# Forward substitution in the RWKV scan of a bidirectional hybrid encoder layer: one series of VectorE operations for two blocks of tokens

## The chip, the cores and the metric

The kernel runs on one core of a Trainium2 chip. A core has five engines that run on their own: TensorE (PE; its weight loads are shown apart as PEld), VectorE (DVE), ScalarE (ACT), GpSimd (POOL) and SyncE (SP). Each works off its own list of instructions in order. DMAs are issued by SP, ACT and POOL and run beside the engines. The metric is the device time of one execution in microseconds (us); lower is better.

## The reference, cut to what matters

One layer of an encoder over 1024 tokens of width 1024, all in float32: half-step SwiGLU feed-forward, a mixing layer, a second half-step feed-forward. The mixing layer projects the tokens once, gives eight heads to a dilated attention and eight heads to an RWKV-7 recurrence that runs over the tokens forward and backward. Only the recurrence bears on the change:

```python
def _rwkv7_step(state, inp):
    r, w, k, v, kk, kka = inp
    sa = jnp.einsum('dbhvk,dbhk->dbhv', state, kk)
    state = state * w[..., None, :] - sa[..., :, None] * kka[..., None, :] + v[..., :, None] * k[..., None, :]
    y = jnp.einsum('dbhvk,dbhk->dbhv', state, r)
    return state, y
...
    _, ys = lax.scan(_rwkv7_step, state0, xs)      # 1024 steps, both directions
    y = ys[:, :, 0] + jnp.flip(ys[:, :, 1], axis=1)
```

The state is 64 by 64 for each head and direction. Then each head is normalised, a bonus is added, the result is gated, and it is joined with the attention for the output projection.

## The kernel before, in words

The kernel is written against a layer that takes the program in the order in which Python issues it, gives each tile a buffer of its pool (a pool has so many buffers for each tag, and a tile waits for the readers of the buffer's last owner), and then orders the instructions of each engine by priority, which follows the program's order, and by when its own model of the times holds them ready. So an engine's list mixes instructions of several steps, and on the chip it is worked off in order.

Feed-forward 1, the input projection and the attention come first, then the scan stage (about 1240 to 1640 us of the execution), then the output projection and feed-forward 2.

The scan is cut in 16 chunks of 64 tokens for each direction; two chunks make a block, so there are 8 blocks of 128 tokens (`NB`). Both directions and eight heads of a block are worked on together. Four steps make a block n:

- `prep` (L783): for each direction it loads the block's decay, in-context rates and projections, takes exponentials (L805, L806 on ACT), forms the products `pr` (L810, L811) and `bk` (L814 to L822) on DVE, multiplies them on PE (L830) and masks the result into `lm` on DVE (L832, eight instructions to a block). `lm` holds the triangular matrices of the block. Four DMAs on SP write the two 32 by 32 diagonal pieces of each to a scratch tensor in DRAM (L846), in an order in which partition means one matrix.
- `solve` (L850): two DMAs on SP load them into `X`, 128 matrices on 128 partitions, each 32 by 32 (L856). POOL clears `Ti` and sets its diagonal (L860, L862). Then 31 steps of forward substitution invert all of them: each step is a multiply (L866) and a subtract (L868) on DVE over r x m elements to a partition, r = 31 - s, m = s // 2 + 1; each waits for the one before. A copy (L870) makes the transpose in `X`, and four DMAs on POOL write both to DRAM (L872, L873).
- `merge` (L875): six DMAs on POOL bring the inverses back in the layout of the matrices (L883, L886), PE multiplies them with the off-diagonal pieces (L894, L900) and ACT copies the result to `tt` (L902).
- `chain` (L918): the sequential part. For each of the two chunks PE multiplies with the carried state (L941, L952, L937), DVE scales the new state (L968), and ACT copies the outputs `yb` (L970), which are stored at the end (L972). The last L970 of a block ends its chain.

The tiles that `prep` hands on (`lm`, `gc`, `pr`, `bt`) come from two pools: `B0` with two buffers for blocks 1, 2, 4, 5 and 7, and `R0` with one for blocks 0, 3 and 6. So block n + 3 takes the buffers of block n, and its `pr` (L810) and `lm` wait for the last matmul of block n's chain. `X`, `Ti` and the scratch tile `ttmp` have two buffers each.

The order in which the program issues the steps is in `run`: block 0's `prep` and `solve`, then `upto(1)` (prep and solve of block 1), the merge of block 0, `upto(2)`, and then for each block n: merge, chain, `upto(n + 3)`, and the output products of the attention for one tile of tokens (`project_attended`, L1066: loads and a multiply L1072, a split L1078, 24 matmuls L1064). Where the scan ends, `finish_unit` (L975) takes over: it adds the directions, normalises and gates.

Of the kernel before, what the change touches and what calls it, by code (L numbers as in the profile page):

```python
# [10 lines left out]
F32 = mybir.dt.float32  # L11
F32R = mybir.dt.float32r
AF = mybir.ActivationFunctionType
OP = mybir.AluOpType
# [17 lines left out]
def _ap(src, off, pat):  # L32
    return bass.AP(tensor=src.tensor, offset=src.offset + off, ap=pat)
# [3 lines left out]
class _GateUp:  # L37
# [3 lines left out]
    def __init__(self, K, ring, rows, w, hid, wd, ws):  # L41
        self.K, self.ring, self.rows, self.w, self.hid, self.wd, self.ws = K, ring, rows, w, hid, wd, ws
        self.A, self.S, self.P, self.X, self.H = {}, {}, {}, {}, {}
        self.ready, self.done = {}, set()
# [38 lines left out]
    def gather(self, n, j):  # L83
# [3 lines left out]
        if n == 1:  # L87
            self.X[j] = [self.rows.tile([128, 2, 512], F32, name="row", tag="row") for q in range(2)]
        x, y = self.X[j]
        if n == 1:  # L90
# [73 lines left out]
class _Kernel:  # L164
# [454 lines left out]
    def far(self, psum, p, h, q, k, v3):  # L619
# [8 lines left out]
        s = p.tile([128, NT, 64], F32, name="sb3", tag="sb3", bufs=1)  # L628
        V.tensor_reduce(out=n3[:, :, 64], in_=ps, op=OP.max, axis=AX.X)
        V.tensor_tensor(s, ps, n3[:, :, 64:65].to_broadcast([128, NT, 64]), op=OP.subtract)  # L630
        A.activation(s, s, AF.Exp)
        V.tensor_reduce(out=n3[:, :, 65], in_=s, op=OP.add, axis=AX.X)
        yield
# [34 lines left out]
    def near(self, psum, p, h, sq, kh, kl, v, far, between):  # L668
# [67 lines left out]
        G.tensor_tensor(f3, y, y, op=OP.mult)  # L736
        V.tensor_reduce(out=self.ss_a[:, :, h], in_=f3, op=OP.add, axis=AX.X)
        self.nc.scalar.dma_start(_ap(self.ya_d, h * 64, [[512, 128], [128 * 512, NT], [1, 64]]), y)
# [108 lines left out]
                                  lm[r0:r0 + 32, par, :, :, :, k * 32:k * 32 + 32].rearrange("p d i a t -> p (d i a) t"))  # L847
        return blk

    def solve(self, n, p):  # L850


        nc, V, G = self.nc, self.nc.vector, self.nc.gpsimd
        X = p.tile([128, 32, 32], F32, name="X", tag="X", bufs=2)
        for q in range(2):
            self.load(X[q * 64:q * 64 + 64].rearrange("p a b -> p (a b)"), self.x_d[n % 4])  # L856
        Ti = p.tile([128, 32, 16], F32, name="Ti", tag="Ti", bufs=2)
        tmp = p.tile([128, 144], F32, name="ttmp", tag="ttmp", bufs=2)
        tf = Ti.rearrange("p a b -> p (a b)")
        G.memset(tf, 0.0)  # L860
        for q in range(2):
            G.memset(tf[q * 64:q * 64 + 64, q * 16:512:33], 1.0)  # L862
        for s in range(31):
            r, m = 31 - s, s // 2 + 1
            tv = tmp[:, :r * m].rearrange("p (a b) -> p a b", a=r)
            V.tensor_tensor(tv, X[:, s, s + 1:][:, :, None].to_broadcast([128, r, m]),  # L866
                            Ti[:, s, 0:m][:, None, :].to_broadcast([128, r, m]), op=OP.mult)
            V.tensor_tensor(Ti[:, s + 1:, 0:m], Ti[:, s + 1:, 0:m], tv, op=OP.subtract)  # L868
        Tt = X[:, 0:16, :]
        V.tensor_copy(Tt, Ti.rearrange("p a b -> p b a"))  # L870
        for q in range(2):
            self.nc.gpsimd.dma_start(_ap(self.t_d[n % 4], q * 16, [[1024, 32], [32, 32], [1, 16]]), Ti[q * 64:q * 64 + 32])  # L872
            self.nc.gpsimd.dma_start(_ap(self.tt_d[n % 4], q * 32, [[1024, 64], [64, 16], [1, 32]]), Tt[q * 64:q * 64 + 64])  # L873

    def merge(self, n, blk, p, psum):  # L875

# [286 lines left out]
    def run(self):  # L1163
# [5 lines left out]
        with self.top as top:  # L1169
# [8 lines left out]
            with ExitStack() as st:  # L1178
# [18 lines left out]
                for t in natural:  # L1197
                    a, b = xr[t % 4], xr[t % 4 + 4]
# [19 lines left out]
                p = self.pool(st, "ffn1")  # L1218
# [40 lines left out]
            NB, s_sr, s_pr, s_zr = NC_ // BLK, ExitStack(), ExitStack(), ExitStack()  # L1259
            pp = self.pool(s_pr, "ps_p", 3, space=PSUM, **R)  # L1260
            sp = self.pool(s_sr, "prep", 1, **R)
# [2 lines left out]
            zr, pz = self.pool(s_zr, "zr", 2), self.pool(s_zr, "ps_r", 1, space=PSUM)  # L1264
            self.project_rwkv(zr, pz, x, [(4, 2), (6, 2), (1, 1), (2, 2)])
            blk = {0: self.prep(0, sp, pp, R0)}
            self.solve(0, sp)
            self.project_rwkv(zr, pz, x, [(8, 2), (10, 2)])
            s_zr.close()
            s_xn.close()  # L1270
# [12 lines left out]
            def upto(m):  # L1283
                while nxt[0] <= min(m, NB - 1):
                    n = nxt[0]
                    blk[n] = self.prep(n, sp, pp, B0 if n % 3 else R0)
                    self.solve(n, sp)
                    nxt[0] += 1

            upto(1)  # L1290
            rs_a = self.rstd(eo, self.ss_a.rearrange("p a b -> p (a b)"), NT * H, 1.0 / HD, EPS)
            self.merge(0, blk[0], sc, pm)
            upto(2)
            WA = self.out_weights(eo, 0, self.aog)
            for n in range(NB):
                if n:
                    self.merge(n, blk[n], sc, pm)
                self.chain(n, blk.pop(n), sc, pc)
                upto(n + 3)
                for t in ([0, 1] if n == 0 else [n + 1] if n + 1 < NT else []):  # L1300
                    self.project_attended(eo, sc, pe, t, WA, rs_a)
# [28 lines left out]
            for j in range(2):  # L1330
                for n in (1, 2):
                    gate_up.ready[n, j] = self.halves(wf, self.slab(wf, gate_up.source(j, 0, n - 1), bufs=2, queue=nc.gpsimd),
                                                      bufs=4)
# [37 lines left out]
            with ExitStack() as st:  # L1371
# [12 lines left out]
                p, hand = self.pool(st, "ffn2"), self.pool(st, "hand3")  # L1384
# [49 lines left out]
```

## Time and profile before

| what | value |
|---|---|
| median of 3 runs (lowest to highest) | 2419.5 us (2416.11 to 2422.34) |
| the profiled execution's own time | 2416.97 us |
| its span, first to last instruction | 2415.2 us, so 1.8 us lie around it |
| mean granted TensorE clock | 0.944 of full speed |
| PE busy | 2244.4 us (93%), 14532 matmuls |
| DVE busy | 1780.8 us (74%), 2917 instructions |
| ACT busy | 1030.2 us (43%) |
| POOL busy | 571.2 us (24%) |
| series of forward substitution (L866 and L868) | 8, each 62 instructions on DVE |

How to read what follows. In a timeline a row gives the start in us, the busy time in us, the engine, the line of the kernel, the operation, `out<-in`, the shape, and how many instructions the row merges; in brackets stands the engine's idle time just before and what ended it. SPq and ACTq are queues that issue DMAs. In a table of windows each engine has its busy us and its number of instructions, PEclk is the mean clock granted to TensorE. A row of waits gives who waited for whom, the sum in us, how often, and the longest. In a table of groups the columns after the bar are busy us, mean ns of one, and idle time before.

### The profile page before, as it was taken

The page shows a single profiled execution, that of the slowest core. Times are in us where ns is not written, and L with a number is a line of the kernel's source. Part 1 is how long each engine was busy: PE and PEld are TensorE (multiplying, and loading weights), DVE is VectorE, ACT ScalarE, POOL GpSimd, SP SyncE. Part 2 cuts the span into 40 slices and gives each one's busy share as a digit, 9 for nine tenths or more (in the row PEclk, how much of TensorE's full clock was granted, in tenths as well). Part 3 has the DMA queues.
Part 4 walks back from the last instruction along what each step waited for, and adds up shares of the span by engine and source line. Part 5 has one row for each costly group of instructions (what it writes and reads, how often), then busy time and mean ns, then how long its engine had stood idle before and what let it go on. Part 6 is the DMA issues. An engine that isn't in the chain of part 4 may idle for free. (4 is left out here: it accounts for less than half of the span.)

```text
span 2415.2 us, 39328 instructions
## 1 busy us (share of the span) xinstructions
PE 2244.4 (93%) x14532; PEld 1812.9 (75%) x14532; DVE 1780.8 (74%) x2917; ACT 1030.2 (43%) x1918; POOL 571.2 (24%) x668
## 2 busy tenths in 40 slices
PE   5999999999999998999987698888879999999997
PEld 4788888788786777778766576765768888887886
DVE  8899999865764446666566767635889999997565
ACT  4322323354676205566445354434542223335453
POOL 6254344400000010111101211222134443432000
PEclk8999999999999998999986688888989999999999
DMA  5354544575643315222366766457445445448655
GB/s 153 105 173 151 172 164 147 199 245 192 211 151 153 143 43 162 83 84 65 99 179 175 171 159 167 133 160 241 163 135 178 172 153 170 152 160 267 193 187 183
DMA packets 359764, 386.03 MB, mean 160 GB/s; under 512 B 73618, under 2 KB 268050, under 8 KB 359572
## 3 DMA queue, kind: packets, MB, share of 16 engines
q1 hardware_dynamic: 314272, 289.02, 39.5%
q0 software_dynamic: 27248, 86.05, 9.6%
q10 hardware_dynamic: 18052, 8.46, 1.3%
q8 instruction: 114, 1.87, 0.3%
q14 instruction: 78, 0.64, 0.1%
HBM read 257.53 MB, written 125.89 MB: 159 GB/s over the span
## 5 line engine op out<-in xcount | busy, mean ns | idle before, releaser
L187 DVE TENSOR_TENSOR wl<-raw,wh 128x512 fp32r<-128x512 f32 (+1 forms) x273 | 277.3, 1019 | 6.0 <-ACT wh L186 5.1
L186 ACT ACTIVATE wh<-raw 128x512 fp32r<-128x512 f32 (+1 forms) x273 | 167.7, 626 | 265.0 <-DVE raw L62 88.5
L81 PE MATMUL gu<-xh,wh 128*128 128x512 f32 x704 | 277.3, 394 | 1.2 <-ACT xh L186 0.8
L81 PE MATMUL gu<-xl,wh 128*128 128x512 f32 x704 | 275.7, 392 | 0.0
L81 PE MATMUL gu<-xh,wl 128*128 128x512 f32 x704 | 275.5, 391 | 0.0
L415 PE MATMUL pd<-gl,gwh 128*128 128x512 f32 x616 | 240.6, 391 | 2.6 <-DVE gl L187 2.6
L415 PE MATMUL pd<-gh,gwh 128*128 128x512 f32 x616 | 239.7, 390 | 0.6 <-DVE row L86 0.6
L415 PE MATMUL pd<-gh,gwl 128*128 128x512 f32 x616 | 239.9, 389 | 0.0
L86 DVE TENSOR_TENSOR row<-gu,row 128x512 f32<-128x512 f32 x308 | 206.9, 684 | 22.7 <-PE gu L81 22.1
L187 DVE TENSOR_TENSOR gwl<-graw,gwh 128x512 fp32r<-128x512 f32 (+1 forms) x176 | 118.1, 674 | 128.1 <-ACT gwh L186 124.1
L116 POOL DMA_DIRECT2D d_hid<-row x154 | 84.7, 551 | 471.6 <-DVE row L114 445.2
L186 ACT ACTIVATE gwh<-graw 128x512 fp32r<-128x512 f32 (+1 forms) x176 | 101.3, 576 | 189.5 <-PE pd L415 156.2
L81 PEld LDWEIGHTS gu<-xh,wh 128*128 128x128 f32 x704 | 133.3, 189 | 30.1 <-ACT xh L186 2.0
L81 PEld LDWEIGHTS gu<-xh,wl 128*128 128x128 f32 x704 | 133.1, 189 | 27.6
L81 PEld LDWEIGHTS gu<-xl,wh 128*128 128x128 f32 x704 | 133.1, 189 | 27.4
L415 PEld LDWEIGHTS pd<-gl,gwh 128*128 128x128 f32 x616 | 115.7, 188 | 28.1 <-DVE gl L187 4.3
L415 PEld LDWEIGHTS pd<-gh,gwh 128*128 128x128 f32 x616 | 115.6, 188 | 25.1 <-DVE row L86 1.0
L415 PEld LDWEIGHTS pd<-gh,gwl 128*128 128x128 f32 x616 | 115.7, 188 | 23.9
L187 DVE TENSOR_TENSOR gl<-raw,gh 128x512 fp32r<-128x512 f32 x160 | 112.4, 714 | 15.9 <-ACT gh L186 15.4
L94 ACT ACTIVATE row<-row 128x512 f32<-128x512 f32 x44 | 27.9, 633 | 225.2 <-DVE row L86 217.7
L145 POOL TENSOR_TENSOR ws<-ws 128x512 f32<-128x512 f32 x88 | 114.2, 1298 | 1.1
L186 ACT ACTIVATE gh<-raw 128x512 fp32r<-128x512 f32 x160 | 98.1, 622 | 32.8 <-DMA raw<-in_ffn_w_down_dram 16.9
(354 smaller groups left out, 5377.7 us busy)
## 6 DMA issues: line engine op xcount, KB each, us to landing
d_hid<-row POOLq DMA_DIRECT2D x154, 256.0 KB, 2.4
graw<-d_hid SPq DMA_DIRECT2D x132, 256.0 KB, 3.0
raw<-in_ffn_w_gate_dram SPq DMA_DIRECT2D x88, 256.0 KB, 3.1
raw<-in_ffn_w_up_dram SPq DMA_DIRECT2D x88, 256.0 KB, 3.4
ws<-in_ffn_w_down_dram SPq DMA_DIRECT2D x88, 256.0 KB, 4.5
d_ws<-ws POOLq DMA_DIRECT2D x88, 256.0 KB, 2.3
raw<-d_ws SPq DMA_DIRECT2D x88, 256.0 KB, 2.8
raw<-in_ffn_w_down_dram SPq DMA_DIRECT2D x66, 256.0 KB, 3.4
```

What stands on the lines that cost most here:

```text
L81: self.K.nc.tensor.matmul(ps, a[:, k, :], b[:, k, :], start=(k == 0 and i == 0), stop=(k == 3 and i == 2))
L86: add = lambda o, x: V.tensor_tensor(o, ps, x, op=OP.add)
L94: A.activation(y[:, 0], y[:, 0], AF.Silu)
L116: put = lambda n, y: G.dma_start(self.hid[n - 1, j // 2], y)
L145: G.tensor_tensor(o, a, b, op=OP.subtract)
L186: self.nc.scalar.activation(h, src, AF.Copy)
L187: (eng or self.nc.vector).tensor_tensor(l, src, h, op=OP.subtract)
L415: T.matmul(ps[x], a[:, ts], b, start=(m == 0 and k == 0), stop=(m == NM - 1 and k == 2))
```

## The change

`solve` takes a list of one or two blocks. `X` and `Ti` get a dimension for the block, with one buffer in place of two (so the memory is the same), and the scratch tile is twice as wide, with one buffer. Each of the 62 instructions works on both blocks, twice the elements. The copies and the DMAs stay one set to a block. The solves are called for block 0 alone, for the pairs 1 and 2, 3 and 4, 5 and 6 as soon as the second one's `prep` is issued, and for block 7 alone: five series in place of eight. `upto(2)` moves ahead of the merge of block 0. `prep`, `merge` and `chain` are not touched.

```diff
-    def solve(self, n, p):
+    def solve(self, ns, p):
...
-        X = p.tile([128, 32, 32], F32, name="X", tag="X", bufs=2)
+        nb = len(ns)
+        X, Ti = (p.tile([128, 2, 32, w], F32, name=c, tag=c)[:, :nb] for c, w in (("X", 32), ("Ti", 16)))
+        tmp = p.tile([128, 2 * 144], F32, name="ttmp", tag="ttmp")
+        for b, n in enumerate(ns):
+            for q in range(2):
+                self.load(X[q * 64:q * 64 + 64, b].rearrange("p a b -> p (a b)"), self.x_d[n % 4])
...
         for s in range(31):
             r, m = 31 - s, s // 2 + 1
-            tv = tmp[:, :r * m].rearrange("p (a b) -> p a b", a=r)
-            V.tensor_tensor(tv, X[:, s, s + 1:][:, :, None].to_broadcast([128, r, m]),
-                            Ti[:, s, 0:m][:, None, :].to_broadcast([128, r, m]), op=OP.mult)
-            V.tensor_tensor(Ti[:, s + 1:, 0:m], Ti[:, s + 1:, 0:m], tv, op=OP.subtract)
-        Tt = X[:, 0:16, :]
-        V.tensor_copy(Tt, Ti.rearrange("p a b -> p b a"))
...
+            tv = tmp[:, :nb * r * m].rearrange("p (n a b) -> p n a b", n=nb, a=r)
+            V.tensor_tensor(tv, X[:, :, s, s + 1:][:, :, :, None].to_broadcast([128, nb, r, m]),
+                            Ti[:, :, s, 0:m][:, :, None, :].to_broadcast([128, nb, r, m]), op=OP.mult)
+            V.tensor_tensor(Ti[:, :, s + 1:, 0:m], Ti[:, :, s + 1:, 0:m], tv, op=OP.subtract)
+        for b, n in enumerate(ns):
+            Tt = X[:, b, 0:16, :]
+            V.tensor_copy(Tt, Ti[:, b].rearrange("p a b -> p b a"))
...
                 while nxt[0] <= min(m, NB - 1):
                     n = nxt[0]
                     blk[n] = self.prep(n, sp, pp, B0 if n % 3 else R0)
-                    self.solve(n, sp)
+                    if n % 2 == 0 or n == NB - 1:
+                        self.solve([n] if n == NB - 1 else [n - 1, n], sp)
                     nxt[0] += 1
 
-            upto(1)
+            upto(2)
             rs_a = self.rstd(eo, self.ss_a.rearrange("p a b -> p (a b)"), NT * H, 1.0 / HD, EPS)
             self.merge(0, blk[0], sc, pm)
-            upto(2)
```

More of the change, by code (lines that the diff above doesn't have):

```diff
@@ L848, in prep @@
         return blk
-    def solve(self, n, p):
+    def solve(self, ns, p):
         nc, V, G = self.nc, self.nc.vector, self.nc.gpsimd
-        X = p.tile([128, 32, 32], F32, name="X", tag="X", bufs=2)
-        for q in range(2):
[L856 to L862, printed above, removed]
+        nb = len(ns)
[4 more added lines that the diff above has]
+                self.load(X[q * 64:q * 64 + 64, b].rearrange("p a b -> p (a b)"), self.x_d[n % 4])
+        tf = Ti.rearrange("p n a b -> p n (a b)")
+        G.memset(Ti.rearrange("p n a b -> p (n a b)"), 0.0)
+        for q in range(2):
+            G.memset(tf[q * 64:q * 64 + 64, :, q * 16:512:33], 1.0)
@@ L863, in solve @@
         for s in range(31):
             r, m = 31 - s, s // 2 + 1
-            tv = tmp[:, :r * m].rearrange("p (a b) -> p a b", a=r)
-            V.tensor_tensor(tv, X[:, s, s + 1:][:, :, None].to_broadcast([128, r, m]),
-                            Ti[:, s, 0:m][:, None, :].to_broadcast([128, r, m]), op=OP.mult)
-            V.tensor_tensor(Ti[:, s + 1:, 0:m], Ti[:, s + 1:, 0:m], tv, op=OP.subtract)
-        Tt = X[:, 0:16, :]
[L870 to L873, printed above, removed]
+            tv = tmp[:, :nb * r * m].rearrange("p (n a b) -> p n a b", n=nb, a=r)
@@ new lines, in solve @@
+            V.tensor_tensor(tv, X[:, :, s, s + 1:][:, :, :, None].to_broadcast([128, nb, r, m]),
[4 more added lines that the diff above has]
+            V.tensor_copy(Tt, Ti[:, b].rearrange("p a b -> p b a"))
+            for q in range(2):
+                self.nc.gpsimd.dma_start(_ap(self.t_d[n % 4], q * 16, [[1024, 32], [32, 32], [1, 16]]),
+                                         Ti[q * 64:q * 64 + 32, b])
+                self.nc.gpsimd.dma_start(_ap(self.tt_d[n % 4], q * 32, [[1024, 64], [64, 16], [1, 32]]),
+                                         Tt[q * 64:q * 64 + 64])
@@ L1266, in run @@
             blk = {0: self.prep(0, sp, pp, R0)}
-            self.solve(0, sp)
+            self.solve([0], sp)
             self.project_rwkv(zr, pz, x, [(8, 2), (10, 2)])
```

## Prediction

> **What bounds the kernel now.** I read the page first, for where the stage of the change lies and what it waits on.
>
> ```profile
> span 2415.2 us, 39328 instructions
> DVE  8899999865764446666566767635889999997565
> PEclk8999999999999998999986688888989999999999
> ```
>
> A digit stands for 60.4 us. Digits 22 to 26 (1268 to 1570 us) lie in the scan: VectorE is at 6 or 7 tenths there, against 8 and 9 in the feed-forwards, and the granted TensorE clock has its lowest digits here. VectorE is not full in this stage. The table of windows says more:
>
> ```profile
> 1320.00:1360.00 40.00, 21.69 (x282) 19.31 (x281) 36.02 (x123) 15.53 (x29) 7.82 (x13) 0.67 0.82 191
> 1400.00:1440.00 40.00, 38.20 (x635) 31.18 (x632) 20.74 (x51) 23.20 (x43) 7.87 (x13) 0.81 0.62 153
> 1395.50:1521.50 126.00, 110.65 (x1768) 92.71 (x1765) 87.23 (x248) 62.18 (x117) 23.44 (x39) 0.84 0.64 165
> 1521.50:1632.90 111.40, 97.59 (x1585) 80.02 (x1582) 52.16 (x151) 44.83 (x82) 20.45 (x25) 0.82 0.51 148
> ```
>
> Columns: window, length, then PE, PEld, DVE, ACT, POOL. VectorE is full only at 1320 to 1360 (36.02 of 40 us), where the solves of blocks 1 and 2 run. The last two windows hold three blocks each and have VectorE at 69% and 47%, TensorE at 88%. What sets their length is seen in the list of waits (first row) and the timelines of VectorE and ScalarE (the others).
>
> ```profile
> DVE pr L810 <- PE y L937: 5.2, 2, 3.0
> 1394.84 0.65 ACT L970 COPY yb<-y 128x256 f32<-128x256 f32 x2 [2.17 <-PE y L937]
> 1417.63 1.29 DVE L832 TENSOR_TENSOR lm<-lp,k_tri 128x512 f32<-128x512 f32 x2 [0.44 <-PE lp L830]
> 1429.83 0.19 DVE L866 TENSOR_TENSOR ttmp<-X,Ti 128x31 f32<-128x31 f32 x1
> 1471.12 0.59 DVE L870 COPY X<-Ti 128x512 f32<-128x512 f32 x1
> 1506.44 1.19 ACT L902 ACTIVATE tt<-pb 32x512 f32<-32x512 f32 x2 [3.08 <-PE pb L900]
> 1520.83 0.65 ACT L970 COPY yb<-y 128x256 f32<-128x256 f32 x2 [2.25 <-PE y L937]
> 1632.22 0.65 ACT L970 COPY yb<-y 128x256 f32<-128x256 f32 x2 [1.44 <-PE y L937]
> ```
>
> The first row is a wait: `pr` of block n + 3 waits for the chain of block n, whose buffers it takes. The next six are one turn: chain 1 ends at 1395.5, prep of block 4 ends at 1418.9, its solve runs from 1429.8, its copy ends at 1471.7, its merge at 1507.6, its chain at 1521.5. The last is chain 7's end at 1632.9. So **the stage is a loop of latencies through three sets of buffers**: 126.0 us for the turn from chain 1 to chain 4, 111.4 from 4 to 7, three blocks in each, some 40 us to a block.
>
> **What the change saves.** A series is a chain of dependent instructions; four rows of VectorE's timeline give its price, and two more show two solves that run together.
>
> ```profile
> 1254.30 0.30 DVE L868 TENSOR_TENSOR Ti<-Ti,ttmp 128x136 f32<-128x136 f32 x1
> 1254.63 0.29 DVE L866 TENSOR_TENSOR ttmp<-X,Ti 128x128 f32<-128x128 f32 x1
> 1266.40 0.18 DVE L866 TENSOR_TENSOR ttmp<-X,Ti 128x16 f32<-128x16 f32 x1
> 1266.61 0.17 DVE L868 TENSOR_TENSOR Ti<-Ti,ttmp 128x16 f32<-128x16 f32 x1
> ...
> 1334.86 0.39 DVE L866 TENSOR_TENSOR ttmp<-X,Ti 128x31 f32<-128x31 f32 x2 [0.48 <-DMA X<-d_x]
> 1335.16 0.41 DVE L868 TENSOR_TENSOR Ti<-Ti,ttmp 128x31 f32<-128x31 f32 x2
> ```
>
> From start to start it is 0.33 us at 136 elements and 0.21 at 16: 1.0 ns an element and 0.194 us fixed. The 62 instructions of a solve hold 2 x 2856 elements (the sum of r x m): 12.0 + 5.7 = 17.7 us when nothing comes between. A pair costs 12.0 + 11.4 = 23.4, where two singles cost 35.4. Three pairs save 36.0 us of VectorE's chains, and 186 instructions go. But the solve in the turn above took 41.3 us, not 17.7, since other steps' instructions and their waits lie in the same list. Part of the fixed time was filled already: in the last two rows the solves of blocks 1 and 2 alternate, and two instructions start every 0.30 us or so.
>
> **What the change adds: a wait.** The first block of a pair now waits for the prep of the second, which waits for a chain. Solve 3 waits for prep 4, so for chain 1; chain 3 needs solve 3. Solve 5 waits for prep 6, so for chain 3; chain 5 needs it. Before, chain 3 hung on chain 0 and chain 5 on chain 2. The turn now carries two blocks, not three, and only chain 2 (or 4) runs beside it. The terms of a turn need more rows of the same timelines:
>
> ```profile
> 1479.00 0.65 ACT L970 COPY yb<-y 128x256 f32<-128x256 f32 x2 [4.34 <-PE y L937]
> 1496.58 0.69 DVE L832 TENSOR_TENSOR lm<-lp,k_tri 128x512 f32<-128x512 f32 x1 [0.26 <-PE lp L830]
> 1514.00 0.19 DVE L866 TENSOR_TENSOR ttmp<-X,Ti 128x31 f32<-128x31 f32 x1
> 1547.22 0.62 DVE L870 COPY X<-Ti 128x512 f32<-128x512 f32 x1
> 1567.32 1.19 ACT L902 ACTIVATE tt<-pb 32x512 f32<-32x512 f32 x2 [0.27 <-PE pb L900]
> 1594.49 0.65 ACT L970 COPY yb<-y 128x256 f32<-128x256 f32 x2 [2.17 <-PE y L937]
> 1554.97 0.19 DVE L866 TENSOR_TENSOR ttmp<-X,Ti 128x31 f32<-128x31 f32 x1
> 1580.03 0.60 DVE L870 COPY X<-Ti 128x512 f32<-128x512 f32 x1
> ```
>
> The first six are block 6 (after chain 3's end at 1479.7), the last two solve 7.
>
> 1. Chain's end to the last `lm`: 23.4 us (block 4), 17.6 (block 6). I take 19: no solve stands in VectorE's list during it any more, but the other block's prep and chain 2 do.
> 2. Last `lm` to the first instruction of the solve (store, load): 10.9 (block 4), 16.7 (block 6, from 1497.3). I take 11.
> 3. The pair's series: 23.4 alone. Solve 7 took 25.1 where 17.7 are its own, 7.4 over; solve 4 lost 23.6. So 23.4 to 47.0; I take 33, nearer to solve 7, because by then most of the other prep is done.
> 4. The copy of the first block, 0.6.
> 5. Copy to the end of the merge (six loads, two rounds on TensorE): 35.9 (block 4), 20.7 (block 6, to 1568.5). POOL issues four stores for the second block ahead of the first block's loads, and they fit into a wait:
>
> ```profile
> 1471.38 0.77 POOL L872 DMA_DIRECT2D d_t<-Ti  x1 [55.89 <-DVE Ti L868]
> 1473.69 0.88 POOL L873 DMA_DIRECT2D d_tt<-X  x1
> 1476.74 0.53 POOL L860 MEMSET Ti<- 128x512 f32 x1 [2.17 <-DMA d_t<-Ti]
> ```
>
> Four stores take 3.2 us from first to last end, then POOL idles 2.17 us for their landing; the other four hide 2.2 of 3.2, so 1 us more. I take 27.5, toward the lower end, because TensorE has less beside it then.
> 6. Merge to the chain's end: 13.9 (block 4), 26.6 (block 6, which waits for a chain before it). Chain 3's predecessor is long done; I take 15.
>
> Sum: 19 + 11 + 33 + 0.6 + 27.5 + 15 = **106.1 us for two blocks**, ends 87 and 150, against about 81 now.
>
> **To the end.** The first pair starts when block 2's `X` is there, 1334.9 as now. Chain 1 then ends at 1334.9 + 33 + 0.6 + 27.5 + 15 = 1411.0 (now 1395.5). Chain 3: 1517.1. The last stretch is set by block 7: `X` and `Ti` have one buffer now, so its load waits for the pair's stores. The view of tile `X` gives what a load takes:
>
> ```profile
> DMA to landing us min/median/max: 3.0/4.2/8.2
> ```
>
> From chain 3 the pair ends after 19 + 11 + 33 = 63; stores land 5.0 later (1471.7 to 1476.7 above); the load takes 4.2. Then 25 for the solve as now, 0.6, 27.5 and 15: 140.3 in all, so chain 7 ends at 1657.4 where it ended at 1632.9, **24.5 us later**. Chain 5 ends at 1623.2, so blocks 5, 6 and 7 fit before that. The queues that the moved steps pass: SP's loads of `X` for two blocks go out together (four issues of about 0.6 us), later than now; the waiting load of block 7 can hold up state loads behind it by a few us, which I leave in the range. `upto(2)` ahead of merge 0 costs nothing as long as block 1's solve is out of VectorE's way then; if not, chain 0 and prep 3 are late by some us. Behind chain 7 the output stage is unchanged and waits for it as now.
>
> The profiled execution took 2417.0 us; 2417 + 24.5 = **2441.5**. The median of the runs, 2419.5, is 0.1% above that execution, within which I do not correct.
>
> TensorE's clock: 0.67 in the window in which it was busy for 21.69 of 40 us, 0.81 where it was busy for 38.20. The turn now has longer stretches with little for TensorE, so the merge and chain behind each pair may run at the lower clock; the some 10 us of matmuls in them would be 2 us longer for each of two turns, 4 us. I leave that in the range. [...]
>
> **Rivals.**
> - *VectorE's series are the path* (faster). If the three pairs' 36.0 us lay on the path in full and the new wait were hidden, the time is 2417 - 36 = 2381. For it: 36.02 of 40 us at 1320 to 1360, and solves that take longest of all terms. Against: VectorE is idle for 31% and 53% of the two turns, and the solve starts later by construction. Needed: a turn of under 95 us. Chance 0.13. [...]
> - *TensorE paces the stage* (no change). It is busy for 88% of both turns; if its list fills the new wait with other blocks' work, the end moves by less than 7 us, 2410 to 2424. Against: with two blocks in a turn there is less to fill with. Chance 0.14.
> - *In-order lists get in the way as for block 4* (far slower). If the pair loses 23.6 us and the merge takes 35.9, a turn is 23.4 + 10.9 + 47.0 + 0.6 + 35.9 + 13.9 = 131.7; chain 1 ends at 1432, chain 3 at 1564, chain 7 another 23.4 + 10.9 + 47.0 + 5.0 + 4.2 + 25 + 0.6 + 35.9 + 13.9 = 165.9 later at 1730, 97 us late: 2514. It decides from a pair's series of over 42 us. Chance 0.10.
>
> **How the numbers follow.** My forecast has 0.63, slower by 8 to 60 us. A measurement of this kernel tells about 0.3%, 7 us. Slower by more: 0.63 + 0.10 = 0.73; within: 0.14; faster: 0.13. The range, 2412 to 2482, holds the forecast, nearly all of no change and a little of the far slower case, and leaves out the faster one.
>
> **What would show it.** Right: five series; a pair's series at 30 to 37 us; chain 3 ending near 1517 and chain 5 near 1623; VectorE's busy time less by some 20 us while idle time grows; first `lm` of block 6 just after chain 3. Wrong: chain 3 before 1490, or a turn of under 95 us, which would mean that the terms shrink when fewer blocks are in flight; or a solve of the first of a pair that does not wait for the second's prep.

## The result, and the profile after

The changed kernel takes 2482.96 us (median of 4 runs, 2474.13 to 2487.53); beside it the kernel before took 2417.81 (median of 4, 2405.53 to 2422.34). The ratio is 1.0275, with a 95% interval of 1.0251 to 1.03: 65 us slower, where 24.5 were forecast. The profiled execution of the changed kernel took 2474.13 us, the fastest of its four, against 2416.97: the traces hold 57.2 us of the difference. Where the other 8 us of the median went is open, since only that one execution was traced.

The changed kernel's lines are numbered a little higher: the series is L867 and L869 now, its copy L872, the merge's last copy L906, the chain's matmul L941 and its output copy L974, the attention's 24 output matmuls L1068. First the page, then the table of windows, by the turns that the prediction named (PE, PEld, DVE, ACT, POOL, then PEclk, the DMA share and GB/s):

```profile
span 2471.9 us, 39159 instructions
DVE  8899999855772546676466362635789999997565
PEclk8999999999999998999966677689989999999999
```

```profile
1408.00:1517.40 109.40, 80.61 (x1180) 66.50 (x1178) 54.68 (x121) 41.68 (x78) 15.43 (x23) 0.72 0.51 131
1517.40:1625.20 107.80, 80.44 (x1178) 66.48 (x1176) 67.41 (x177) 37.00 (x69) 17.69 (x27) 0.72 0.42 108
1439.10:1482.60 43.50, 31.54 (x330) 25.48 (x330) 34.99 (x88) 13.74 (x27) 0.00 (x0) 0.72 0.53 146
1625.20:1686.50 61.30, 52.89 (x962) 42.46 (x955) 11.55 (x20) 26.66 (x49) 10.76 (x12) 0.89 0.57 173
```

A turn, from one pair's last chain to the next pair's, takes 109.4 and 107.8 us and carries two blocks. Before, turns of 126.0 and 111.4 us carried three. TensorE is busy for 74% of a turn (80.61 of 109.40), where it was for 88%, and its granted clock fell from 0.84 and 0.82 to 0.72. VectorE has lost 186 instructions (2917 to 2731) and only 14.3 us of busy time over the whole kernel (1780.8 to 1766.5); it is idle more, not less.

The ends of chains 1, 3, 5, 6 and 7, in ScalarE's timeline:

```profile
1407.35 0.65 ACT L974 COPY yb<-y 128x256 f32<-128x256 f32 x2 [2.17 <-PE y L941]
1516.74 0.65 ACT L974 COPY yb<-y 128x256 f32<-128x256 f32 x2 [2.17 <-PE y L941]
1624.60 0.65 ACT L974 COPY yb<-y 128x256 f32<-128x256 f32 x2 [2.17 <-PE y L941]
1653.46 0.65 ACT L974 COPY yb<-y 128x256 f32<-128x256 f32 x2 [2.17 <-PE y L941]
1685.82 0.65 ACT L974 COPY yb<-y 128x256 f32<-128x256 f32 x2 [1.28 <-PE y L941]
```

Start plus busy time: chain 1 ends at 1408.0 (forecast 1411.0), chain 3 at 1517.4 (1517.1), chain 5 at 1625.2 (1623.2). Then the forecast fails: chain 7 ends at 1686.5, not at 1657.4. It ended at 1632.9 before, so it is 53.6 us late, and what comes behind it takes 785.4 us to the end of the span, where it took 782.3. These two make 56.7 of the 57.2 us.

### The profile page after: what moved, and what is told of

Its sections match the earlier page's. It is cut to its first block, busy times and chain, and to the rows that moved or that the text cites. A ratio compares the mean times of both kernels' runs of the same rounds, so it can differ in the third digit from the quotient of the medians.

```text
span 2471.9 us, 39159 instructions
## 1 busy us (share of the span) xinstructions
PE 2251.6 (91%) x14532; PEld 1819.4 (74%) x14532; DVE 1766.5 (71%) x2731; ACT 1030.6 (42%) x1918; POOL 571.8 (23%) x659
## 5 line engine op out<-in xcount | busy, mean ns | idle before, releaser
L187 DVE TENSOR_TENSOR gl<-raw,gh 128x512 fp32r<-128x512 f32 x160 | 112.6, 715 | 14.5 <-ACT gh L186 14.3
L186 ACT ACTIVATE gh<-raw 128x512 fp32r<-128x512 f32 x160 | 98.0, 621 | 32.8 <-DMA raw<-in_ffn_w_down_dram 19.8
```

What stands on the lines that cost most here:

```text
L186: self.nc.scalar.activation(h, src, AF.Copy)
L187: (eng or self.nc.vector).tensor_tensor(l, src, h, op=OP.subtract)
```

## The experiments

**Theory.** The first block of a pair waits for the `prep` of the second, which waits for buffers that a chain frees. So the loop through three sets of buffers carries two blocks in nearly the time that it needed for three. **Rivals:** the order of the program or the lists cost the time, without the wait; the wide form does; the single buffer of `X` and `Ti` does; TensorE paces the stage; VectorE's series are the path.

**1. The order of the change, with the old series** (e1_wait_only). Every block has its own series and `X`, `Ti` and `ttmp` have two buffers, as before; only the calls come in the order of the pairs:

```diff
-                    self.solve(n, sp)
+                    if n % 2 == 0 or n == NB - 1:
+                        for k in [n] if n == NB - 1 else [n - 1, n]:
+                            self.solve(k, sp)
...
-            upto(1)
+            upto(2)
...
-            upto(2)
```

> The solve of the kernel before (62 instructions for each block, two buffers for X, Ti and ttmp), but called in pairs: blocks 1 and 2, 3 and 4, 5 and 6 when the second one's prep is issued, upto(2) ahead of merge 0. So the wait alone, without wide instructions and without the single buffer. Theory (the first of a pair waits for the second's prep, and so for a chain): the turn from chain 1 to chain 3 stays near 108 us, chain 3 ends at 1505 to 1525, chain 5 at 1610 to 1635, the whole 2455 to 2485 us. Rival (the wide instructions or the single buffer cost the time, the order does not): about 2418, chain 3 near 1480.

2414.01 us (median of 10) beside 2414.59 for the kernel before; 0.9993 [0.997, 1.0016]. The expectation failed, and the rival's number came: the order costs nothing. VectorE's timeline in this kernel shows why, by the first instruction of solve 3 and the first `lm` of block 4 behind it:

```profile
1381.34 0.19 DVE L866 TENSOR_TENSOR ttmp<-X,Ti 128x31 f32<-128x31 f32 x1 [6.36 <-DMA X<-d_x]
...
1395.74 1.29 DVE L832 TENSOR_TENSOR lm<-lp,k_tri 128x512 f32<-128x512 f32 x2
```

Solve 3 starts 14 us ahead of prep 4's `lm`, although the program issues it later. Nothing in its data makes it wait, and the layer orders the lists also by when its model holds an operation ready. So this kernel had the order and not the wait; it clears the order, and the wait had to be built into the data (experiment 5).

**2. Other pairs** (e2_odd_pairs): 0 and 1 alone, then 2 with 3, 4 with 5, 6 with 7.

```diff
-                    if n % 2 == 0 or n == NB - 1:
-                        self.solve([n] if n == NB - 1 else [n - 1, n], sp)
+                    if n == 1 or n % 2:
+                        self.solve([n] if n == 1 else [n - 1, n], sp)
```

> The changed kernel with the pairs shifted by one: blocks 0 and 1 alone, pairs 2 and 3, 4 and 5, 6 and 7. Same number of series, same instructions. Theory (a turn of about 108 us from an even chain to the next): chain 0 ends near 1325, chain 2 near 1435, chain 4 near 1543, chain 6 near 1651, chain 7 some 30 later, and no solve waits alone for the single buffer at the end: 2455 to 2478, slower than before by 40 to 60. Rival (the wide form itself is slow): the same 2483 as the changed kernel.

2484.12 us (median of 4); 1.0273 [1.0238, 1.0307]: the same as the changed kernel. The expectation was missed by 6 us, and the number is the one that the rival had forecast. By ScalarE's timeline chain 2 already ended at 1453.0, 18 us later than expected; the two turns behind it took 209.4 us together, where 216 were reckoned. Which blocks make a pair does not matter, and as wait and wide form are both in this run, it can't tell them apart.

**3 and 4. The attention's output products two tiles earlier**, in the changed kernel (e3_after_early) and in the kernel before (e4_before_early):

```diff
-                for t in ([0, 1] if n == 0 else [n + 1] if n + 1 < NT else []):
+                for t in ([0, 1, 2, 3] if n == 0 else [n + 3] if n + 3 < NT else []):
```

> The changed kernel with the attention's output products issued two tiles of tokens earlier (four behind chain 0, none behind chains 5 and 6). Theory for the last stretch (chain 5 to chain 7 took 61.3 us, not 34, because TensorE was filled with these products): the stretch shrinks to 35 to 48 us, the whole to 2455 to 2472. Rival (the last solve, which waits for the single buffer, sets it): within 7 us of 2483.

> The kernel before with the attention's output products issued two tiles of tokens earlier. Theory (a loop of latencies; TensorE only matters in the last stretch): 2400 to 2415, with chain 4's end about where it was (1521) or later. Rival (TensorE, busy for 88% of a turn, paces the stage): the products go into the time at 1320 to 1360 when TensorE is half idle, 20 us of work leaves the later turns, 2395 to 2403.

The changed kernel so edited took 2475.73 us (median of 4); 1.0236 [1.019, 1.0281]. That lies between what the theory (up to 2472) and the rival (2476 or more) expected, and its interval overlaps that of the changed kernel. Chains 5 and 7 in ScalarE's timeline:

```profile
1650.99 0.65 ACT L974 COPY yb<-y 128x256 f32<-128x256 f32 x2 [2.18 <-PE y L941]
...
1695.58 0.65 ACT L974 COPY yb<-y 128x256 f32<-128x256 f32 x2 [2.17 <-PE y L941]
```

From chain 5 to chain 7 it takes 44.6 us, against 61.3 with the products in their old place: without these products the last stretch is 17 us shorter. But chain 5 ends 26 us later (1651.6 against 1625.2), since the products now lie in the turns, which take 113 and 116.5 us. The work only moved. The kernel before, so edited, took 2418.46 (median of 10), 0.9994 [0.9966, 1.0022], a little above the expected band and far from the rival's. But it does not test that rival: the products did not go into the time at 1320 to 1360 (TensorE was busy there for 20.36 of 40 us, before for 21.69). They delayed chain 1 by 14 us (1409.8 against 1395.5) and made the stretch from chain 4 to chain 7 12.5 us shorter (98.9 against 111.4). Whether TensorE paces the stage is decided by experiments 8 and 12.

**5. The wait alone** (e5_forced_wait). Two series of the old form, two buffers, and one VectorE instruction of 16 elements that adds nothing but reads the second block's `X` and writes the first block's `Ti`:

```diff
+        if len(ns) > 1:
+            V.scalar_tensor_tensor(Tis[0][:, 0, :], Xs[1][:, 0, 0:16], 0.0, Tis[0][:, 0, :], op0=OP.mult, op1=OP.add)
```

> Pairs in which the wait is real but the instructions are not wide: two series of 62 instructions with two buffers as before, and one VectorE instruction of 16 elements that adds 0 times a row of the second block's X to the first block's Ti, so that the first series can't start before the second block's X is there. The run called wait_only had no such dependence, so its lists could start the first series early, and it showed 1.000. Theory (the dependence on the second block closes a loop that carries two blocks in place of three): as slow as the changed kernel or some us less, since the last solve needn't wait for the single buffer: 2455 to 2490, turn from chain 1 to chain 3 of 100 to 115 us. Rival (the wide instructions or the single buffer cost the time): 2415, turn of about 83.

2469.33 us (median of 4) beside 2411.3; 1.0232 [1.0201, 1.0263]: 58 us slower, without the wide form and without the single buffer. Chains 1, 3, 5 and 7:

```profile
1413.48 0.65 ACT L977 COPY yb<-y 128x256 f32<-128x256 f32 x2 [2.17 <-PE y L944]
1518.28 0.65 ACT L977 COPY yb<-y 128x256 f32<-128x256 f32 x2 [2.17 <-PE y L944]
1620.05 0.65 ACT L977 COPY yb<-y 128x256 f32<-128x256 f32 x2 [2.17 <-PE y L944]
1678.44 0.65 ACT L977 COPY yb<-y 128x256 f32<-128x256 f32 x2
```

Turns of 104.8 and 101.8 us and a last stretch of 58.4: the pattern of the changed kernel. As `X` and `Ti` have two buffers here, the single buffer makes little of the last stretch either (61.3 in the changed kernel). VectorE's timeline shows what the wide form could still have saved here, with two series ready together; the last row is the last step of the later one:

```profile
1452.83 0.18 DVE L867 SCALAR_TENSOR_TENSOR Ti<-X,Ti 128x16 f32<-128x16 f32 x1 [0.46 <-DMA X<-d_x]
1453.04 0.29 DVE L873 TENSOR_TENSOR ttmp<-X,Ti 128x31 f32<-128x31 f32 x2
1453.27 0.39 DVE L875 TENSOR_TENSOR Ti<-Ti,ttmp 128x31 f32<-128x31 f32 x2
1453.56 0.32 DVE L873 TENSOR_TENSOR ttmp<-X,Ti 128x30 f32<-128x30 f32 x2
...
1454.04 0.35 DVE L873 TENSOR_TENSOR ttmp<-X,Ti 128x58 f32<-128x58 f32 x2
1454.30 0.34 DVE L875 TENSOR_TENSOR Ti<-Ti,ttmp 128x58 f32<-128x58 f32 x2
...
1476.33 0.17 DVE L875 TENSOR_TENSOR Ti<-Ti,ttmp 128x16 f32<-128x16 f32 x1
```

Each row marked x2 merges two instructions, one of either block. At 31 elements a step of both blocks takes 0.52 us (1453.04 to 1453.56), and the two series together end after 23.5 us (1453.04 to 1476.50), with a few instructions of other steps between. The prediction reckoned 35.4 for two lone series and 23.4 for a lone wide one. The order of the list had already put one block's instruction into the other's latency; in this kernel the wide form has nothing left to save.

**6. The wide form for each block alone** (e6_wide_alone). The second half is a copy of the same block, one buffer, and it is stored once; the calls stand as in the kernel before:

```diff
-        for b, n in enumerate(ns):
+        for b, n in enumerate(ns[:1]):
...
+                    self.solve([n, n], sp)
```

> The wide form without the wait: each block has its own series, and the second half of X holds the same block once more (loaded twice, stored once). Eight series of 62 wide instructions, 23.4 us each when alone in place of 17.7, one buffer for X, Ti and ttmp. Theory (the wait costs the time): 2412 to 2440, since 5.7 us more lie in each of three turns at most. Rival (the wide form or the single buffer is what costs): 2465 or more.

2519.61 us (median of 4); 1.045 [1.0419, 1.0481]: the expectation was missed by 80 us, and the result lies in the rival's band: wide form and single buffer together can cost a kernel more than the whole change did. Two blocks in VectorE's timeline:

```profile
1422.60 0.68 DVE L872 COPY X<-Ti 128x512 f32<-128x512 f32 x1
...
1437.52 0.22 DVE L867 TENSOR_TENSOR ttmp<-X,Ti 128x62 f32<-128x62 f32 x1 [8.68 <-DMA X<-d_x]
...
1481.25 0.61 DVE L872 COPY X<-Ti 128x512 f32<-128x512 f32 x1
...
1497.59 0.22 DVE L867 TENSOR_TENSOR ttmp<-X,Ti 128x62 f32<-128x62 f32 x1 [12.27 <-DMA X<-d_x]
```

There is a second loop, which the expectation left out: series, stores, load into the same buffer, next series. From copy to the next series it takes 14 to 16 us, the series itself 44 with other steps between, some 58 us to a block where the stage gives a block 40. In the changed kernel a pair has a turn of 108 us, more than such a loop would need (a series of 38 to 44 us, then 14 to 16), and the series at 1439.12 and 1548.20 (rows below) start without a wait for their `X`. So by these rows the loop decides only the start of block 7 there, behind the last pair.

**7. One buffer with the old series** (e7_one_buffer):

```diff
-        X = p.tile([128, 32, 32], F32, name="X", tag="X", bufs=2)
+        X = p.tile([128, 32, 32], F32, name="X", tag="X")
-        Ti = p.tile([128, 32, 16], F32, name="Ti", tag="Ti", bufs=2)
-        tmp = p.tile([128, 144], F32, name="ttmp", tag="ttmp", bufs=2)
+        Ti = p.tile([128, 32, 16], F32, name="Ti", tag="Ti")
+        tmp = p.tile([128, 144], F32, name="ttmp", tag="ttmp")
```

> The kernel before with one buffer for X, Ti and ttmp in place of two, nothing else. Theory (the wait for the second block costs the time): a solve now waits for the stores of the one before it and the load, some 12 us, but the loop has slack only where two solves overlap (blocks 1 and 2): 2412 to 2430. Rival (the single buffer is what costs): 2450 or more.

2440.24 us (median of 4); 1.0113 [1.0082, 1.0145], 10 us above the expected band. By itself the lost second buffer costs 29 us, with one series to a block. This can't be added to the wait's 58: the two would make 87, and the change costs 65. That fits loops that run beside each other, of which the longer one decides; no run shows it directly.

**8. A shorter series without any wait** (e8_short_series):

```diff
-        for s in range(31):
+        for s in range(16):
```

> The kernel before with 16 of the 31 steps (leaves out the other 15, so the inverses are incomplete): 32 instructions, 9.3 us alone in place of 17.7. It tells what a shorter series is worth when no wait is added. Theory (loop of latencies, three blocks to a turn): 8 to 12 us less in each of two and a half turns, 2388 to 2405. Rival (VectorE's series lie on the path in full): eight times 8.4, some 67 us less, 2350. Rival (TensorE paces the stage): within 7 us of 2415.

2392.77 us (median of 4); 0.9914 [0.9884, 0.9944]. Leaving out 15 of 31 steps of every block gives 19 us, as the theory had it. VectorE's busy time fell by 48.8 us (1780.8 to 1732.0), the end by 19: the series does lie in the loop, but less than half of what it gives up reaches the end. With the same 14532 matmuls the kernel became faster, so TensorE does not set its pace: that rival had it within 7 us of 2415.

**9 to 12. A fourth set of buffers.** A complete kernel with it wasn't tried, and no run shows whether it has room in SBUF (the core's memory for tiles) beside the attention's output weights. Instead the two kernels were made slim first (e9_slim_before, e10_slim_after), with one weight tile for all of the attention's output product and one tile for both parts of the other factor, which leaves out the product's right values but none of its matmuls. Then they were given a fourth set (e11_slim_after_4sets, e12_slim_before_4sets):

```diff
-                h = p.tile([128, 512], F32R, name="woh", tag="woh", bufs=8)
-                l = p.tile([128, 512], F32R, name="wol", tag="wol", bufs=8)
+                h = p.tile([128, 512], F32R, name="woh", tag="woh", bufs=8 if gain is None else 1)
+                l = p.tile([128, 512], F32R, name="wol", tag="wol", bufs=8) if gain is None else h
...
-            B0 = self.pool(s_sc, "blks", 2)
+            B0 = self.pool(s_sc, "blks", 3)
...
-                    blk[n] = self.prep(n, sp, pp, B0 if n % 3 else R0)
+                    blk[n] = self.prep(n, sp, pp, B0 if n % 4 else R0)
```

> The kernel before with one weight tile for all of the attention's output products (the first one, its high part in place of all high and low parts, and one tile for both parts of the factor; so that product's values are left out, its 24 matmuls to a tile of tokens stay). It frees 32 KB of SBUF. It is the base for the next three. Seven of eight weight loads and splits go. Every theory: 2395 to 2415.

> The changed kernel with the same one weight tile as the run slim_before. Every theory: slower than slim_before by as much as the change was, 50 to 75 us.

> The run slim_after with a fourth set of buffers for lm, pr, bt and gc (block n takes the buffers of block n - 4). The pair 3 and 4 then waits for chain 0, not chain 1, and a turn carries three blocks as it did before the change. Theory (the wait for the second block's buffers is the cost): within 20 us of slim_before, so 40 us or more come back. Rival (the wide form, the single buffer, or the wait for the second prep's own work is the cost): within 15 us of slim_after.

> The run slim_before with the fourth set of buffers. Theory (three sets close the loop before the change too, and TensorE, at 88%, is next): 10 to 30 us less than slim_before. Rival (TensorE paces the stage already): within 7 us of slim_before.

| kernel | us | ratio to the kernel before (2410.59) |
|---|---|---|
| slim, before (median of 10) | 2409.75 | 0.9993 [0.9971, 1.0014] |
| slim, after (4) | 2476.62 | 1.0269 [1.0233, 1.0305] |
| slim, after, four sets (4) | 2443.44 | 1.0121 [1.0082, 1.016] |
| slim, before, four sets (4) | 2387.82 | 0.9901 [0.9866, 0.9935] |

Slimming changes nothing in the time. The fourth set gives the pairs 33 of their 67 us back, fewer than the theory's 40, more than its rival's 15. But it also makes the kernel before 22 us faster: three sets close a loop there too, only a less tight one. This again speaks against TensorE as the pace, whose rival had it within 7 us. Against its own counterpart the pair still costs 56 us with four sets (2443.44 - 2387.82), 67 with three. The profile of the pairs with four sets has a candidate for what is left: prep 4's `lm`, SP's loads of `X` for blocks 3 and 4, the start of their series and chain 1's end, then what SP waited for from 1380 to 1400 us.

```profile
1362.87 0.68 DVE L832 TENSOR_TENSOR lm<-lp,k_tri 128x512 f32<-128x512 f32 x1
...
1396.37 2.39 SPq L182 DMA_DIRECT2D X<-d_x  x4
...
1404.58 0.22 DVE L867 TENSOR_TENSOR ttmp<-X,Ti 128x62 f32<-128x62 f32 x1 [17.09 <-DMA X<-d_x]
...
1421.96 0.65 ACT L974 COPY yb<-y 128x256 f32<-128x256 f32 x2 [2.17 <-PE y L941]
```

```profile
SPq L182 <- DMA d_tt<-X: 8.2, 2, 6.5
```

Prep 4 now runs well ahead of chain 1's end: the old wait is gone. Yet the pair's series starts at 1404.6, 20.5 us after its matrices lay in DRAM (the last `d_x` store landed at 1384.1). The first pair's copies ended at 1387.5. The last store of its `X` was issued at 1392.5 and landed 3.5 to 3.8 us later, and only then could the loads go out, at 1396.4. So the next loop in line is the single buffer, the one of experiment 6. That it makes up all that is left wasn't shown: two buffers and four sets together weren't tried. Of the complete kernels none was faster than the kernel before.

## Why the prediction was wrong, point by point

The direction and the mechanism were right: slower, by the wait for the second block's `prep`. The wait alone, without the wide form and the single buffer, costs 58 us (experiment 5), the whole change 65, and the order without the wait nothing (experiment 1). The 7 us between are no more than the two intervals leave open. The rivals fell. VectorE's series are not the path (experiment 8: 19 us for 15 of 31 steps), and TensorE does not pace the stage (experiments 8 and 12: 19 and 22 us faster with the same matmuls). The far slower rival was to decide from a pair's series of over 42 us. One series took 43.5, but the merge behind it took 18.6 us in place of that rival's 35.9, so its turn did not come.

**The steps up to chain 5 held in sum, partly by luck: two errors cancel.** These rows of the changed kernel hold the first pair's series (start and copies) and the first turn (the last `lm` of block 4, the start of the series, its copies, the merge's last copy; DVE first, then ACT):

```profile
1339.05 0.22 DVE L867 TENSOR_TENSOR ttmp<-X,Ti 128x62 f32<-128x62 f32 x1 [0.56 <-DMA X<-d_x]
1373.03 1.09 DVE L872 COPY X<-Ti 128x512 f32<-128x512 f32 x2
1426.87 1.29 DVE L832 TENSOR_TENSOR lm<-lp,k_tri 128x512 f32<-128x512 f32 x2 [0.44 <-PE lp L830]
1439.12 0.22 DVE L867 TENSOR_TENSOR ttmp<-X,Ti 128x62 f32<-128x62 f32 x1
1482.64 1.09 DVE L872 COPY X<-Ti 128x512 f32<-128x512 f32 x2
```

```profile
1500.59 1.19 ACT L906 ACTIVATE tt<-pb 32x512 f32<-32x512 f32 x2 [1.55 <-PE pb L904]
```

| term of the turn | forecast | 1408.0 to 1517.4 | 1517.4 to 1625.2 |
|---|---|---|---|
| 1, chain to the last `lm` | 19 | 20.2 | 19.8 |
| 2, to the series | 11 | 10.9 | 11.0 |
| 3, the pair's series | 33 | 43.5 | 38.2 |
| 4, copy | 0.6 | 0.6 | 0.6 |
| 5, to the end of the merge | 27.5 | 18.6 | 22.6 |
| 6, chain | 15 | 15.6 | 15.6 |
| sum | 106.1 | 109.4 | 107.8 |

The first pair's series took 34.0 us; both series of the turns lie outside the 30 to 37 us that were to show the forecast right. In the window of the first of these two, 1439.10 to 1482.60 above, VectorE is busy for 34.99 of 43.50 us with 88 instructions, and 62 of them are the series: the next `prep` runs in the same list. The merge, in turn, takes 18.6 to 22.6 us, under its 27.5; that it finds lists with less in them by then is likely and was not tested. The price of an instruction was right: at 270 elements two of them start 0.48 us apart in VectorE's timeline, where 0.194 + 0.270 = 0.464 were reckoned:

```profile
1575.02 0.44 DVE L867 TENSOR_TENSOR ttmp<-X,Ti 128x270 f32<-128x270 f32 x1
1575.50 0.44 DVE L869 TENSOR_TENSOR Ti<-Ti,ttmp 128x270 f32<-128x270 f32 x1
```

VectorE lost 14.3 us of busy time, not some 20.

**The step that failed is "To the end": the last stretch, 140.3 us from chain 3 to chain 7, took 169.1.** Its terms in the changed kernel's timelines of VectorE, then of ScalarE:

```profile
1548.20 0.23 DVE L867 TENSOR_TENSOR ttmp<-X,Ti 128x62 f32<-128x62 f32 x1
1586.39 1.09 DVE L872 COPY X<-Ti 128x512 f32<-128x512 f32 x2
1601.20 0.19 DVE L867 TENSOR_TENSOR ttmp<-X,Ti 128x31 f32<-128x31 f32 x1 [13.72 <-DMA X<-d_x]
1621.97 0.59 DVE L872 COPY X<-Ti 128x512 f32<-128x512 f32 x1
```

```profile
1657.79 1.19 ACT L906 ACTIVATE tt<-pb 32x512 f32<-32x512 f32 x2 [0.22 <-PE pb L904]
```

| term | forecast | measured |
|---|---|---|
| chain 3 to the pair's series | 30 | 30.8 |
| the pair's series, with its two copies | 33 | 39.3 |
| stores and the load for block 7 | 9.2 | 13.7 |
| solve 7 with its copy | 25.6 | 21.4 |
| merge 7 | 27.5 | 36.4 |
| chain 7 | 15 | 27.5 |
| sum | 140.3 | 169.1 |

Merge and chain of block 7 are 21.4 of the 28.8 us: 36.4 and 27.5 where 27.5 and 15 were forecast. The prediction gave them the prices of a turn's middle, although its own row 6 had 26.6 us for a chain that waits for another, and block 7 stands behind block 6. The kernel before had a row for the drain itself, the last copy of merge 7 in ScalarE's timeline:

```profile
1609.44 1.20 ACT L902 ACTIVATE tt<-pb 32x512 f32<-32x512 f32 x2 [1.05 <-PE pb L900]
```

Solve 7's copy ended at 1580.63 there, merge 7 at 1610.64 and chain 7 at 1632.87: merge and chain took 30.0 and 22.2 us, not 27.5 and 15. And the forecast let chains 6 and 7 follow chain 5 within 34.2 us; they took 28.9 and 32.4 (1625.2 to 1654.1 to 1686.5). TensorE's timeline shows what lies between (the merge's matmuls are L898 and L904):

```profile
1633.91 1.11 PE L1079 MATMUL yq<-ident,yat 128*128 128x128 f32 x4 [3.11 <-DVE yat L1076]
...
1637.10 0.80 PE L1068 MATMUL po<-woh,yah 128*128 128x512 f32 x1
1637.69 0.63 PE L1068 MATMUL po<-wol,yah 128*128 128x512 f32 x1
...
1644.36 0.39 PE L1068 MATMUL po<-woh,yal 128*128 128x512 f32 x1
...
1646.29 0.69 PE L898 MATMUL pa<-d,lm 32*32 32x32 f32 x30
...
1656.54 1.20 PE L904 MATMUL pb<-tt,d 32*32 32x32 f32 x64
...
1665.91 2.07 PE L999 MATMUL yc<-f_y,k_cen 128*128 128x512 f32 x2
...
1668.54 0.80 PE L1068 MATMUL po<-woh,yah 128*128 128x512 f32 x1
...
1675.45 0.39 PE L1068 MATMUL po<-woh,yal 128*128 128x512 f32 x1
```

Merge 7 begins at 1636.9 and is held up by 24 attention products (1637.1 to 1644.8) and by chain 6 beside them; chain 7 finds the first finish unit's matmul and 24 more products (1668.5 to 1675.8) in the list ahead of its own. Experiment 3, which takes the products out of this stretch, shortens it by 17 us, but chain 5 then ends 26 us later, so moving them saves next to nothing. The rest, 44.6 against 34.2 by the forecast, wasn't taken apart further.

The stores and the load were 4.5 us over, since eight stores on POOL (1586.95 to 1593.50, 6.6 us, where the four took 3.2) stand ahead of the `Ti` clearing (1595.46) and the load (1596.18); that term was priced with the landing of one store after four issues. The clock's 4 us, left in the range, don't show in a term of the turns: the chains at their ends, with the granted clock at 0.76 and 0.71 (1501.78 to 1517.40 and 1609.60 to 1625.20), took 15.6 us where 15 were reckoned. Over the whole execution TensorE's 14532 matmuls were busy for 2251.6 us in place of 2244.4, which speaks for the lower clock (0.932 on the mean, 0.944 before) as a small part of the 57.2 at most.

## What to carry to other kernels

Before merging two short dependent chains into one, see whether the in-order list already puts one into the latency of the other. Where two series were ready together it did (experiment 5): they took 23.5 us together, where 23.4 were reckoned for the merged form. Then ask what the second operand waits for: in a loop through N sets of buffers, a result that needs two blocks at once makes a turn carry fewer (two in place of three here), while the same order of calls without that need in the data cost nothing. And price the drain at a stage's end from rows of the drain, where the engines' lists hold the next stage's work too.

## What the runs showed of the hardware

Where TensorE had less work, its granted clock was lower: 0.72 in turns that it filled to 74%, 0.84 and 0.82 in turns that it filled to 88%. The busy share alone does not set it, since experiment 5 had 0.77 in turns filled to 75%. What the clock means for one instruction stands in TensorE's timeline above. TensorE idled for 3.11 us before 1633.9, and within that time the granted clock fell: it was 1.00 from 1630.8 to 1631.5 us and 0.50 from 1632.5 to 1633.9. It stayed at 0.50 to 1638.9; there the first attention product takes 0.80 us and the next three 0.63. From 1639.3 to 1644.7 it was 1.00, and there the products at the end of the same 24, of the same shape, take 0.39. That is 0.80 to 0.39, about two to one, for the first product, and 0.63 to 0.39, 1.6 to one, for the next three. Whether the idle time alone lowered the clock isn't shown.
